# Gate and up projections of two feed-forwards as seven block products, with gate and down in two phases

## The chip, the cores and the metric

One core of a Trainium2 chip. The metric is device time in microseconds (us) from one launch; lower is better.

## The reference

One step of a small backbone of two layers over 1024 latent tokens and 128 context tokens, width 1024. Layer 0 mixes tokens by differential attention, layer 1 by a long convolution (Hyena). Behind each mixer's output projection stands a feed-forward:

```
h = rmsnorm(x) * g * (1 + scale) + shift
x = x + gate * ((silu(h @ w_g) * (h @ w_u)) @ w_down)
```

with w_g and w_u of 1024 x 2816 and w_down of 2816 x 1024. Everything is float32. scale, shift and gate come from a second set of products ("ada") with the condition vectors, one set for latents, one for context. At the end stands one more rmsnorm.

## The kernel before, in words

Activations lie transposed: 128 partitions hold 128 of the 1024 features, so a tensor is 8 blocks (k) of 1152 tokens. The tokens are worked in NCH = 3 chunks of CH = 384 columns, mostly in the order 2, 0, 1 (`ORDER`); the context is the last 128 columns of chunk 2.

Each float32 operand is split into a high and a low part of the fp32r type, and a product is three matmuls: high x high, high x low, low x high (`three`, L289). `lin` (L294) runs these over the 8 blocks of features: 24 matmuls for one output block of 128 x 384. A weight unit of 512 KB is loaded by `fetch` (L271) into one of two `raw` buffers through SP's queue; ScalarE copies it to the high part (L279) and VectorE subtracts for the low part (L280), three buffers each. `part` (L1311) does the same for other operands, `split` (L462) with GpSimd for the high part.

`project` (L835) is the mixer's output projection: eight output blocks d, for each of the three chunks one `lin` and a `residual` (L824: x += gate * PSUM, on VectorE), followed by the square of x on ScalarE (L398) and its sum over the blocks on GpSimd (L402). The last three units are worked chunk by chunk, and `step` normalises a chunk while the next one is multiplied: `rstd` (L407) sums over partitions on TensorE, takes the square root on ScalarE, refines it in five small VectorE operations, spreads it by three products with a diagonal (L430, L431); `modulate` (L434) multiplies each block with it (L444), scales it on ScalarE (L446) and splits it (L447, L448). The last chunk's step stands inside `ffn`, behind the first products of chunk 2.

`ffn` (L866) runs over the HT = 22 tiles of hidden features. For each tile and chunk `gated` (L1116) makes the gate block and the up block (one `lin` each), silu on ScalarE (L1124), the product on VectorE (L1125) and the split on GpSimd and VectorE (L463, L464). After each second tile the two are multiplied with w_down and the 8 output blocks of each chunk are added to x; the last four tiles are summed in PSUM first. So gate, up and down are interleaved, and activations of the hidden layer never leave SBUF. In layer 0 the ada products of layer 1 (`ada_step`, L344, four loads of 512 KB in two buffers, 32 small matmuls) stand one behind each of the tiles 2 to 13.

The order of instructions on an engine is chosen by a planner of the framework from the program's order and its own estimate of times, SP's queue of DMAs included; `pin` (L632) fixes the program's order on the engines that it names for a stretch. It is used in the attention and in the convolution, not in the feed-forwards.

## Time and profile before

| | us |
|---|---|
| median of three runs | 3223.13 |
| lowest, highest run | 3221.38, 3225.62 |
| span of the profiled execution | 3218.2 |
| TensorE busy in it | 3140.6 |
| VectorE busy | 1702.0 |
| ScalarE busy | 1006.4 |
| GpSimd busy | 672.8 |

The page lists no own time for the profiled execution, so its span stands beside the median of the runs, which is 4.9 us longer. The feed-forward of layer 0 lies at about 985 to 1815 us of the span, that of layer 1 at 2387 to 3200. A matmul's record overlaps the next one's, so its cost is read from the distance of two starts. GpSimd stands as POOL, VectorE as DVE, ScalarE as ACT, TensorE as PE and its weight loads as PEld.

### The profile page before, as it was taken

Reading aid. Unit: us, or ns where it says so; the run is one execution under the profiler, and the core shown is the slowest. Engines: PE = TensorE matmul, PEld = TensorE weight load, DVE = VectorE, ACT = ScalarE, POOL = GpSimd, SP = SyncE. Lnnn points to the kernel's source line nnn. Section 1 sums busy time; section 2 is a strip of 40 time slices with the busy share of each in tenths; the row PEclk is TensorE's granted clock in tenths of the full one; section 3 lists DMA queues with packets and bytes.
Section 4 is the critical chain, followed back from the end, with each engine's and each line's share of the span. In section 5 each row is a group of like instructions: output and inputs, shape, how many; then the busy total and the mean of one; then the engine's idle time right before and its main releaser. Section 6 shows DMA issues by size and latency. Waiting matters only on the chain.

```text
span 3218.2 us, 49673 instructions
## 1 busy us (share of the span) xinstructions
PE 3140.6 (98%) x20266; PEld 3069.1 (95%) x20266; DVE 1702.0 (53%) x2902; ACT 1006.4 (31%) x1892; POOL 672.8 (21%) x739
## 2 busy tenths in 40 slices
PE   6899999999999999999999999999999999999998
PEld 5779989999999999999999999999999999999998
DVE  7866524989736333333432578875453344444324
ACT  3541124888624111111111442335451111111114
POOL 5844401444332000000000413132230000000003
PEclk9899999999999999999999999999999999999999
DMA  6565452444211222222111233345401111111111
GB/s 251 203 217 178 139 161 63 101 97 101 92 40 60 92 92 92 92 92 79 40 53 40 101 118 114 124 169 196 141 34 46 40 47 46 40 40 40 51 42 66
DMA packets 123084, 308.13 MB, mean 96 GB/s; under 512 B 12991, under 2 KB 65607, under 8 KB 118760
## 3 DMA queue, kind: packets, MB, share of 16 engines
q1 hardware_dynamic: 107480, 282.58, 26.7%
q10 hardware_dynamic: 13968, 17.65, 1.6%
q0 software_dynamic: 1408, 4.72, 0.4%
q8 instruction: 160, 2.62, 0.3%
q14 instruction: 68, 0.56, 0.1%
HBM read 243.56 MB, written 61.34 MB: 95 GB/s over the span
## 4 chain that ended last, share of the span: by engine, by line
PE 88%; DMA 4%; DVE 3%; POOL 1%; issue 1%; ACT 1%; SPq 0%; ACTq 0%; POOLq 0%; DVEq 0%
PE mm L290 25%; PE mm L291 25%; PE mm L292 25%; PE tr L770 4%; PE sc L744 2%; PE sc L745 2%; PE tr L761 2%; PE tr L353 1%; DMA zt<-d_z 1%; DVE wl L915 1%; PE tr L292 1%; PE tr L290 1%; PE tr L291 1%; DMA pr<-d_p 0%; DMA kk<-d_k 0%
## 5 line engine op out<-in xcount | busy, mean ns | idle before, releaser
L291 PE MATMUL mm<-hl,wh 128*128 128x384 f32 x3408 | 1140.2, 335 | 0.9 <-DVE hl L507 0.8
L290 PE MATMUL mm<-hh,wh 128*128 128x384 f32 x3408 | 1137.8, 336 | 2.4 <-ACT hh L506 1.8
L292 PE MATMUL mm<-hh,wl 128*128 128x384 f32 x3408 | 1137.3, 335 | 0.0
L290 PEld LDWEIGHTS mm<-hh,wh 128*128 128x128 f32 x3408 | 639.7, 188 | 8.1 <-ACT hh L506 2.7
L291 PEld LDWEIGHTS mm<-hl,wh 128*128 128x128 f32 x3408 | 640.3, 188 | 4.6 <-issue 1.8
L292 PEld LDWEIGHTS mm<-hh,wl 128*128 128x128 f32 x3408 | 640.2, 188 | 1.9 <-issue 0.4
L279 ACT ACTIVATE wh<-raw 128x1024 fp32r<-128x1024 f32 x194 | 203.5, 1058 | 950.3 <-PE mm L291 827.0
L827 DVE SCALAR_TENSOR_TENSOR x<-mm,ada,x 128x256 f32<-128x256 f32 (+1 forms) x704 | 343.2, 513 | 278.0 <-PE mm L292 276.8
L1125 DVE TENSOR_TENSOR silu<-mm,silu 128x384 f32<-128x384 f32 x132 | 73.5, 557 | 593.9 <-PE mm L292 589.4
L463 POOL TENSOR_SCALAR ah<-silu 128x384 fp32r<-128x384 f32 x132 | 70.3, 533 | 1462.3 <-DVE silu L1125 1449.8
L280 DVE TENSOR_TENSOR wl<-raw,wh 128x1024 fp32r<-128x1024 f32 x194 | 243.9, 1265 | 214.5 <-ACT wh L279 214.3
L291 PE MATMUL mm<-al,wh 128*128 128x384 f32 x1056 | 354.1, 335 | 0.0
L290 PE MATMUL mm<-ah,wh 128*128 128x384 f32 x1056 | 353.8, 335 | 0.0
L292 PE MATMUL mm<-ah,wl 128*128 128x384 f32 x1056 | 353.3, 335 | 0.0
L1124 ACT ACTIVATE silu<-mm 128x384 f32<-128x384 f32 x132 | 64.0, 485 | 440.6 <-PE mm L292 440.6
L291 PEld LDWEIGHTS mm<-al,wh 128*128 128x128 f32 x1056 | 198.3, 188 | 1.4 <-issue 1.2
L290 PEld LDWEIGHTS mm<-ah,wh 128*128 128x128 f32 x1056 | 198.3, 188 | 1.2 <-issue 1.2
L292 PEld LDWEIGHTS mm<-ah,wl 128*128 128x128 f32 x1056 | 198.3, 188 | 0.0
L751 DVE TENSOR_REDUCE nm<-sc 128x1 f32<-128x1152 f32 x128 | 173.5, 1356 | 33.4 <-PE sc L745 33.3
L753 ACT ACTIVATE pr<-sc,nm 128x1152 f32<-128x1152 f32 x128 | 156.7, 1224 | 14.0 <-DVE nm L751 7.7
L402 POOL TENSOR_TENSOR nacc<-nacc,nsq 128x384 f32<-128x384 f32 x104 | 117.0, 1129 | 182.8 <-ACT nsq L398 182.1
L744 PE MATMUL sc<-kk,qs 128*128 128x384 f32 x384 | 140.0, 364 | 3.3 <-ACT pr L753 3.3
(300 smaller groups left out, 4228.0 us busy)
## 6 DMA issues: line engine op xcount, KB each, us to landing
raw<-w_gu SPq DMA_DIRECT2D x88, 512.0 KB, 3.3
araw<-ada_w SPq DMA_DIRECT2D x64, 512.0 KB, 4.1
kk<-d_k SPq DMA_DIRECT2D x16, 1152.0 KB, 8.4
raw<-w_down SPq DMA_DIRECT2D x36, 512.0 KB, 3.7
raw<-w_in SPq DMA_DIRECT2D x24, 512.0 KB, 3.2
hl<-ada_w SPq DMA_DIRECT2D x23, 512.0 KB, 7.4
d_f<-bf ACTq DMA_DIRECT2D x16, 512.0 KB, 2.6
raw<-w_qk SPq DMA_DIRECT2D x16, 512.0 KB, 5.8
```

The lines of the kernel that those rows point to most:

```text
L279: nc.scalar.activation(hi, raw, AF.Copy)
L280: nc.vector.tensor_tensor(out=lo, in0=raw, in1=hi.bitcast(F32), op=ALU.subtract)
L290: self.nc.tensor.matmul(out, ah, bh, start=first, stop=False)
L291: self.nc.tensor.matmul(out, ah, bl, start=False, stop=False)
L292: self.nc.tensor.matmul(out, al, bh, start=False, stop=last)
L402: nc.gpsimd.tensor_tensor(out=self.acc[c], in0=self.acc[c], in1=sq, op=ALU.add)
L744: nc.tensor.matmul(sc[:, c, :CH], lhs, kk[:, 0, p, ks], start=True, stop=False)
L751: nc.vector.tensor_reduce(out=nm, in_=sv, axis=AX.XY, op=ALU.max, negate=True)
L753: nc.scalar.activation(e.rearrange("p (a b) -> p a b", a=3), sv, AF.Exp, bias=nm, accum_out=st[hd][3][:, p, qt : qt + 1])
L770: self.nc.tensor.matmul(po[:, :P], at[:, b], v[:, b], start=b == 0, stop=b == 8)
L827: self.nc.vector.scalar_tensor_tensor(out=x[:, d, s:e], in0=ps[:, s:e], scalar=gate[:, d, g : g + 1], in1=x[:, d, s:e], op0=ALU.mult, op1= ...
L1125: nc.vector.tensor_tensor(out=s, in0=pu[:, :CH], in1=s, op=ALU.mult)
```

## The change

The gate tile and the up tile of one t are taken as the two block rows of a 2 x 2 block matrix (features k 0 to 3 and 4 to 7 are its block columns), and the tokens in two halves of HALF = 576 columns as the block columns of the other factor, k 0 to 3 and 4 to 7 as its block rows. Their product is made by Winograd's form of Strassen's scheme: seven block products instead of eight, each over 4 blocks k and in two parts of SUB = 288 columns, with sums of the weights (on GpSimd, `side_sums`), sums of the tokens (`combos`, once for a feed-forward) and sums of the products (on VectorE, out of PSUM). P1 is the product of the gate's first half with the tokens' first half, and so on, by the numbers in `mul`. The order of TensorE, VectorE, ScalarE and GpSimd is pinned for the whole phase.

x is written to DRAM (`d_r`) by the projection and normalised in place; each hidden tile is written to DRAM (`d_a`). Then a second phase, `down`, loads x and, in groups of 2, 4, 4, 4, 4, 4 tiles, the hidden tiles, splits them and multiplies with w_down. The 12 ada steps go to that phase, one behind each weight unit from the second group on. x is now held in half rows of 576 tokens (16 tiles `xk`), so chunk 1 lies in two of them and its operations are done in two pieces; the output projection takes the chunks in the order 0, 1, 2. The 16 `xk` buffers also serve for the weight sums and the products' sums while gate and up are made, and the space of h serves for the tokens' combinations.

```
+HALF = NT // 2
+SUB = HALF // 2
+GROUPS = [2, 4, 4, 4, 4, 4]
...
+    def open_h(self, tags=("hs", "hs")):
+        self.hstack = ExitStack()
+        self.hp = self.hstack.enter_context(self.pool("h"))
+        self.htags = tags
+
+    def htile(self, shape, dt=F32, which=0):
+        return self.tl(self.hp, shape, dt, tag=self.htags[which], bufs=6 if self.htags[0] == self.htags[1] else 3)
...
     def load_x(self, src):
-        self.x = []
-        for c in range(NCH):
-            t = self.tl(self.xp, [P, KT, CH], tag=f"x{c}")
-            self.nc.sync.dma_start(t, src[c])
-            self.x.append(t)
+        self.xk = []
+        for k in range(KT):
+            self.xk.append([])
+            for h in range(2):
+                t = self.tl(self.xp, [P, HALF], tag="xk", bufs=16)
+                self.nc.sync.dma_start(t, src[k][:, HALF * h : HALF * h + HALF])
...
+        a, sh = self.scales(l, 1)
+        low = [self.operand(bx, f"b{j}") for j in range(2)]
+
+        def step(c):
+            rs = self.rstd(c)
+            for k in range(KT):
+                for x, s, e, _ in self.whole(c, k):
+                    nc.vector.tensor_tensor(out=x, in0=rs[:, s:e], in1=x, op=ALU.mult)
+                for x, s, e, g in self.x(c, k):
+                    nc.scalar.activation(x, x, AF.Identity, scale=a[:, k, g : g + 1], bias=sh[:, k, g : g + 1])
+                if c < 2:
+                    o = slice(0, CH) if c == 0 else slice(CH, HALF)
+                    self.part(*(t[:, k % 4, o] for t in low[k // 4]), self.xk[k][0][:, o])
+
...
+                    for x, s, e, _ in self.whole(c, d):
+                        nc.sync.dma_start(self.d_r[l][d][:, CH * c + s : CH * c + e], x)
+                    if d == 5 and c:
+                        step(c - 1)
...
+    def operand(self, pool, tag):
+        return tuple(self.tl(pool, [P, 4, HALF], F32R, tag=tag + n) for n in "hl")
+
+    def combos(self, low, bx, tp):
+        nc, tt = self.nc, self.tt
+        ADD, SUB = ALU.add, ALU.subtract
+        t1, t2, t3 = (self.operand(tp, f"t{j}") for j in range(1, 4))
+        top = self.operand(bx, "b2")
+        u, v = (self.tl(tp, [P, 4, HALF], tag="t4" + n) for n in "hl")
+        f = lambda t, k: t[:, k].bitcast(F32)
+        b = [self.xk[k][1] for k in range(KT)]
+        self.ops = ops = {1: low[0], 2: low[1], 3: top, 5: t1, 6: t2, 7: t3}
+
+        def second():
+            for k in range(4):
+                tt(u[:, k], b[k], f(low[0][0], k), SUB)
+                tt(u[:, k], u[:, k], f(low[0][1], k), SUB)
+                tt(v[:, k], b[k + 4], u[:, k], SUB)
+                self.part(t2[0][:, k], t2[1][:, k], v[:, k])
+
+        def third():
+            for k in range(4):
+                tt(b[k], b[k + 4], b[k], SUB)
+                self.part(t3[0][:, k], t3[1][:, k], b[k])
+
+        def first():
+            for k in range(4):
+                self.part(t1[0][:, k], t1[1][:, k], u[:, k])
+
+        def fourth():
+            for k in range(4):
+                tt(b[k], f(low[1][0], k), v[:, k], SUB, nc.gpsimd)
+                tt(b[k], b[k], f(low[1][1], k), ADD, nc.gpsimd)
+            t4 = ops[4] = self.operand(tp, "t4")
+            for k in range(4):
+                self.part(t4[0][:, k], t4[1][:, k], b[k])
+
+        def last():
+            for k in range(4):
+                self.part(top[0][:, k], top[1][:, k], b[k + 4])
+
+        return second, third, first, fourth, last
+
+    def side_load(self, l, t):
+        raws = [self.tl(self.wp, [P, 1024], tag="raw", bufs=2) for _ in range(2)]
+        for raw, at in zip(raws, (t, HT + t)):
+            self.nc.sync.dma_start(raw, self.i["w_gu"][l, at])
+        return raws
+
+    def side_sums(self, g, u):
+        nc, tt = self.nc, self.tt
+        ADD, SUB = ALU.add, ALU.subtract
+        s1, s2, s3, s4 = (self.tl(self.xp, [P, 512], tag="xk", bufs=16) for _ in range(4))
+        a11, a12, a21, a22 = g[:, 0:512], g[:, 512:1024], u[:, 0:512], u[:, 512:1024]
+        tt(s1, a21, a22, ADD, nc.gpsimd)
+        tt(s2, s1, a11, SUB, nc.gpsimd)
+        tt(s3, a11, a21, SUB, nc.gpsimd)
+        tt(s4, a12, s2, SUB, nc.gpsimd)
+        return s1, s2, s3, s4
+
+    def side_one(self, x):
+        w = tuple(self.tl(self.xp, [P, 512], F32R, tag="xk", bufs=16) for _ in range(2))
+        self.part(*w, x)
+        return w
+
+    def side_two(self, *src):
+        hi, lo = (self.tl(self.wp, [P, 1024], F32R, tag=n, bufs=3) for n in ("wh", "wl"))
+        for j, y in enumerate(src):
+            c = slice(0, 1024) if len(src) == 1 else slice(512 * j, 512 * j + 512)
+            self.part(hi[:, c], lo[:, c], y)
+        return (hi[:, 0:512], lo[:, 0:512]), (hi[:, 512:], lo[:, 512:])
+
+    def times(self, out, w, b, first):
+        wh, wl = (y.rearrange("p (k c) -> p k c", c=P) for y in w)
+        for k in range(4):
+            for h in range(2):
+                c = slice(SUB * h, SUB * h + SUB)
+                self.three(out[:, h, 0:SUB], wh[:, k], wl[:, k], b[0][:, k, c], b[1][:, k, c], first and k == 0, k == 3, skip_group_check=True)
+
+    def gate_up(self, l, combos):
+        nc, tt, ops = self.nc, self.tt, self.ops
+        st = {t: {"w": {}} for t in range(HT + 1)}
+
+        def raws(t):
+            if t < HT:
+                st[t]["raw"] = self.side_load(l, t)
+
+        def sums(t):
+            if t < HT:
+                st[t]["s"] = self.side_sums(*st[t]["raw"])
+
+        def pair(t, n):
+            if t < HT:
+                w = st[t]["w"]
+                if n == 1:
+                    w[1], w[2] = self.side_two(st[t]["raw"][0])
+                elif n == 2:
+                    w[6], w[7] = self.side_two(*st[t]["s"][1:3])
+                elif n == 3:
+                    w[5], w[3] = self.side_two(*st[t]["s"][0::3])
+                else:
+                    w[4] = self.side_one(st[t]["raw"][1][:, 512:1024])
+
+        def bank():
+            return self.tl(self.pp, [P, 2, 512], tag="pr", bufs=3)[:, :, 0:SUB]
+
+        def work():
+            return self.tl(self.xp, [P, 2, SUB], tag="xk", bufs=16)
+
+        def mul(t, n):
+            q, name, first = st[t], {1: "a", 2: "a", 6: "b", 5: "b", 3: "b", 7: "c", 4: "c"}[n], n in (1, 6, 7)
+            if first:
+                q[name] = bank()
+            self.times(q[name], q["w"][n], ops[n], first)
+
+        def p1(t):
+            mul(t, 1)
+            st[t]["s1"] = work()
+            nc.scalar.activation(st[t]["s1"], st[t]["a"], AF.Copy)
+
+        def p2(t):
+            mul(t, 2)
+            st[t]["g"] = work()
+            nc.scalar.activation(st[t]["g"], st[t]["a"], AF.Silu)
+
+        def p6(t):
+            q = st[t]
+            mul(t, 6)
+            q["v"] = work()
+            tt(q["v"], q["b"], q["s1"], ALU.add)
+
+        def p7(t):
+            q = st[t]
+            mul(t, 7)
+            q["r"] = work()
+            tt(q["r"], q["c"], q["s1"], ALU.add)
+
+        def p5(t):
+            q = st[t]
+            mul(t, 5)
+            tt(q["r"], q["b"], q["r"], ALU.add)
+
+        def p4(t):
+            q = st[t]
+            mul(t, 4)
+            tt(q["v"], q["c"], q["v"], ALU.add)
+            tt(q["v"], q["g"], q["v"], ALU.mult, nc.gpsimd)
+            nc.sync.dma_start(self.d_a[l][t][:, 0:HALF], q["v"].rearrange("p a b -> p (a b)"))
+
+        def p3(t):
+            q = st[t]
+            mul(t, 3)
+            tt(q["s1"], q["b"], q["s1"], ALU.add)
+            nc.scalar.activation(q["s1"], q["s1"], AF.Silu)
+            tt(q["r"], q["s1"], q["r"], ALU.mult, nc.gpsimd)
+            nc.sync.dma_start(self.d_a[l][t][:, HALF:NT], q["r"].rearrange("p a b -> p (a b)"))
+            del st[t]
+
+        second, third, first, fourth, last = combos
+        raws(0), sums(0), pair(0, 1), pair(0, 4), raws(1), pair(1, 1)
+        p1(0), p1(1)
+        pair(0, 2), second()
+        p2(0), p2(1)
+        pair(0, 3)
+        p6(0), third()
+        p7(0), first()
+        p5(0), fourth(), sums(1), pair(1, 2), pair(1, 4), raws(2)
+        p4(0), last()
+        p3(0), pair(1, 3)
+        for t in range(1, HT):
+            if t > 1:
+                pair(t, 3)
+                p1(t)
+            sums(t + 1), pair(t + 1, 4)
+            p6(t)
+            if t > 1:
+                p2(t)
+            p7(t), pair(t + 1, 1)
+            p5(t), pair(t + 1, 2), raws(t + 2) if t + 2 < HT else None
+            p4(t)
+            p3(t)
+
+    def ffn(self, l, after):
+        bx, tp, ps = ExitStack(), ExitStack(), ExitStack()
+        bp = bx.enter_context(self.pool("bx", side="right"))
+        low, step = self.project(l, bp)
+        self.hstack.close()
+        tpool = tp.enter_context(self.pool("tp"))
+        step(NCH - 1)
+        self.mstack.close()
+        self.pp = ps.enter_context(self.pool("psa", space=bass.MemoryType.PSUM))
+        start = len(self.nc.cur_bb.bb.instructions)
+        self.at += 1
+        self.gate_up(l, self.combos(low, bp, tpool))
+        self.pin(start, (ENG.PE, ENG.DVE, ENG.Activation, ENG.Pool))
+        ps.close()
+        self.open_mm()
+        tp.close()
+        bx.close()
+        self.open_h()
+        self.load_x(self.d_r[l])
+        self.bstack = ExitStack()
+        self.ntp = self.sp = self.bstack.enter_context(self.pool(f"ffn{l}", side="right"))
+        return self.down(l, after)
+
+    def down(self, l, after):
         nc = self.nc
         gate = self.gate(l, 1)
...
+        at, ada, step = 0, 0, None
+
+        def load(at, m):
+            act = [self.htile([P, 2, 4, CH], F32R) for c in range(NCH)]
+            for k in range(m):
+                raw = self.tl(self.sp, [P, NT], tag="araw2", bufs=3)
+                nc.sync.dma_start(raw, self.d_a[l][at + k])
+                for c in range(NCH):
+                    self.part(act[c][:, 0, k], act[c][:, 1, k], raw[:, CH * c : CH * c + CH])
+            return act
+
+        acts = [load(0, GROUPS[0])]
+        for n, m in enumerate(GROUPS):
+            last = n == len(GROUPS) - 1
+            act = acts.pop(0)
+            at += m
+            if not last:
+                acts.append(load(at, GROUPS[n + 1]))
+            if last:
+                step = after()
+            per = D * m // 1024
+            for us in ([0], [1, 2, 3]) if last else [[u] for u in range(per)]:
+                ws = self.weights(3) if len(us) == 3 else [self.weights()]
                 for c in ORDER:
...
+                    for u, w in zip(us, ws):
+                        w = [y.rearrange("p (k d) c -> p k d c", k=m) for y in w]
+                        for e in range(8 // per):
+                            d = 8 // per * u + e
+                            ps = self.mm()
+                            for k in range(m):
+                                self.three(ps[:, :CH], w[0][:, k, e], w[1][:, k, e], act[c][:, 0, k], act[c][:, 1, k], k == 0, k == m - 1)
+                            self.residual(ps, d, c, gate, last)
+                            if last and d == 2 and c != ORDER[0]:
+                                step()
+                if l == 0 and n and ada < 12:
+                    self.ada_step(1, ada)
+                    ada += 1
         return step
```

## Rows read from the trace of the kernel before

**Rows 1.** The page: span, then busy time (share) and instructions of each engine.

```profile
span 3218.2 us, 49673 instructions
...
PE 3140.6 (98%) x20266; PEld 3069.1 (95%) x20266; DVE 1702.0 (53%) x2902; ACT 1006.4 (31%) x1892; POOL 672.8 (21%) x739
```

**Rows 2.** Stretches: us, busy (count) by engine, clock, DMA share, GB/s.

```profile
core 0: us, PE busy (x) PEld busy (x) DVE busy (x) ACT busy (x) POOL busy (x), PEclk, DMA share, GB/s
985.00:1790.00 805.00, 804.35 (x5246) 792.80 (x5245) 305.37 (x528) 116.01 (x173) 44.50 (x75) 1.00 0.21 72
2387.00:3155.00 768.00, 768.00 (x4437) 768.00 (x4436) 299.48 (x510) 111.52 (x159) 43.53 (x74) 1.00 0.12 42
...
0.00:200.00 200.00, 161.78 (x1293) 138.15 (x1294) 161.96 (x266) 94.09 (x171) 125.05 (x144) 0.95 0.62 222
```

**Rows 3.** TensorE's waits in 985 to 1815: us, times, longest.

```profile
PE tr L353 <- DMA araw<-ada_w: 0.6, 1, 0.6
```

**Rows 4.** Timeline of TensorE, first down product: start us, us, instruction.

```profile
2599.85 0.33 PE L290 MATMUL mm<-ah,wh 128*128 128x384 f32 x1
...
2601.41 0.33 PE L290 MATMUL mm<-ah,wh 128*128 128x384 f32 x1
```

**Rows 5.** Timeline of TensorE, values projection.

```profile
449.89 0.28 PE L290 MATMUL mm<-wh,hh 128*128 128x256 f32 x1
...
450.97 0.28 PE L290 MATMUL mm<-wh,hh 128*128 128x256 f32 x1
```

**Rows 6.** Groups by line and form, weight loads: busy us, mean ns.

```profile
L290 PEld LDWEIGHTS mm<-hh,wh 128*128 128x128 f32 x3408 | 639.7, 188 | 8.1 <-ACT hh L506 2.7 <-issue 2.2 <-POOL hh L810 1.0
...
L290 PEld LDWEIGHTS mm<-wh,hh 128*128 128x128 f32 x288 | 55.8, 195 | 0.8 <-issue 0.2
```

**Rows 7.** Groups by line and form, VectorE; then its timeline.

```profile
L280 DVE TENSOR_TENSOR wl<-raw,wh 128x1024 fp32r<-128x1024 f32 x194 | 243.9, 1265 | 214.5 <-ACT wh L279 214.3
...
L444 DVE TENSOR_TENSOR nt<-tr,x 128x384 f32<-128x384 f32 x72 | 37.1, 548 | 6.2 <-PE tr L431 3.9 <-POOL hl L448 1.7
...
974.02 1.22 DVE L280 TENSOR_TENSOR wl<-raw,wh 128x1024 fp32r<-128x1024 f32 x1
...
981.50 1.94 DVE L444 TENSOR_TENSOR nt<-tr,x 128x384 f32<-128x384 f32 x4
```

**Rows 8.** Groups by line and form, ScalarE; then its timeline.

```profile
L279 ACT ACTIVATE wh<-raw 128x1024 fp32r<-128x1024 f32 x194 | 203.5, 1058 | 950.3 <-PE mm L291 827.0 <-issue 108.9 <-DMA raw<-w_gu 6.5
...
L447 ACT ACTIVATE hh<-nt 128x384 fp32r<-128x384 f32 x72 | 35.9, 513 | 0.2
...
974.97 0.97 ACT L446 ACTIVATE nt<-nt,ada,A 128x256 f32<-128x256 f32 x2
```

**Rows 9.** Groups by line and form, GpSimd operations with two operands.

```profile
L627 POOL TENSOR_TENSOR pr<-pr,pr 128x384 f32<-128x384 f32 x64 | 63.9, 999 | 5.0
...
L915 POOL TENSOR_TENSOR gt<-zt,gt 128x1024 f32<-128x1024 f32 x7 | 16.8, 2399 | 35.7 <-DVE zt L1360 35.7
```

**Rows 10.** Timeline of VectorE, start of the second feed-forward.

```profile
2396.29 0.16 DVE L420 TENSOR_SCALAR nv<-tr 128x3 f32<-128x3 f32 x1 [1.21 <-ACT nr L419]
...
2397.50 0.48 DVE L430 TENSOR_SCALAR ndg<-ident,nr 128x128 f32<-128x128 f32 x2
...
2403.14 0.56 DVE L444 TENSOR_TENSOR nt<-tr,x 128x384 f32<-128x384 f32 x1 [0.29 <-PE tr L431]
```

**Rows 11.** Timelines of VectorE and GpSimd, start of the first feed-forward.

```profile
975.15 0.55 DVE L448 TENSOR_TENSOR hl<-nt,hh 128x384 fp32r<-128x384 f32 x1
...
978.24 1.38 DVE L448 TENSOR_TENSOR hl<-nt,hh 128x384 fp32r<-128x384 f32 x1
...
978.20 1.01 POOL L402 TENSOR_TENSOR nacc<-nacc,nsq 128x384 f32<-128x384 f32 x1
979.17 1.33 POOL L448 TENSOR_TENSOR hl<-nt,hh 128x384 fp32r<-128x384 f32 x1
```

**Rows 12.** TensorE's longest wait on a load in v(); stretches around it.

```profile
PE aux L600 <- DMA pr<-d_p: 6.7, 1, 6.7
...
438.90:449.20 10.30, 5.82 (x28) 5.59 (x29) 1.41 (x7) 2.34 (x8) 0.00 (x0) 0.50 0.71 210
449.20:460.00 10.80, 10.80 (x91) 10.55 (x91) 1.71 (x8) 2.88 (x11) 0.00 (x0) 1.00 0.20 66
```

**Rows 13.** DMA issues: kernel tile, source, queue, count, KB each, us to landing.

```profile
raw<-w_gu SPq DMA_DIRECT2D x88, 512.0 KB, 3.3
araw<-ada_w SPq DMA_DIRECT2D x64, 512.0 KB, 4.1
...
raw<-w_down SPq DMA_DIRECT2D x36, 512.0 KB, 3.7
```

229 lines of the change are left out of this document (95 added, 134 removed).

## The prediction

> **What bounds the kernel now.** I read the engines' totals first: TensorE is busy for 3140.6 of 3218.2 us, VectorE for 1702 [rows 1]. Then the two feed-forwards by stretch: in 805 us and in 768 us TensorE has practically no gap, while VectorE is busy for under 40%, ScalarE under 15% and GpSimd under 6% [rows 2], and the waits of TensorE in the first of them come to 0.6 us, once [rows 3]. So nothing but matmul time is worth anything there, and any wait that the change puts in front of TensorE is paid in full. What one matmul costs is read from starts, since their durations overlap: nine matmuls of 384 columns lie between 2599.85 and 2601.41 us, 173.3 ns each [rows 4]; nine of 256 columns between 449.89 and 450.97, 120.0 ns each [rows 5]. The difference is 53.3 ns for 128 columns, so a matmul costs 0.4167 ns a column and 13.3 ns besides; 288 columns cost 133.3 ns. A weight load's record is 188 ns at 384 columns and 195 ns at 256 [rows 6], and yet the matmuls of 256 follow each other every 120 ns: loads are no limit there, nor between the two.
>
> **Part 1, seven products for eight.** Before, gate and up are 22 tiles x 2 x 3 chunks x 8 k x 3 = 3168 matmuls of 384 columns for each feed-forward: 549.0 us. After, 22 x 7 products x 4 k x 2 halves x 3 = 3696 matmuls of 288: 492.8 us. The columns fall by an eighth, but 528 matmuls more each bring their 13.3 ns. Saved: 56.2 us, twice, **112.4 us**. The down product keeps its 1584 matmuls of 384 columns: 0.
>
> **Part 2, a tile in the steady state.** One product is 24 x 133.3 ns = 3.2 us, a tile 22.4 us. Prices: VectorE takes 0.55 us for 384 elements and 1.22 to 1.27 for 1024, and 1.94 for four of 384 in a row [rows 7], so about 0.6 for 512 and 0.67 for 576 in a row; ScalarE 0.51 for 384 and 1.06 for 1024 [rows 8], 0.53 and 0.58; GpSimd's two-operand operations 1.00 for 384 and 2.40 for 1024 [rows 9], 1.28 and 1.42. Per tile VectorE has weight splits of 1.2 + 5 x 0.6 and five sums out of PSUM at 0.7: 7.7 us; ScalarE about 6; GpSimd the four weight sums and two gate products, 4 x 1.28 + 2 x 1.42 = 8.0, which it now does in a written order. Each result is needed a product or more (3.2 us) after it can be made. DMA moves 1.6 MB a tile, 73 GB/s; the first 200 us moved 222 GB/s at a share of 0.62 [rows 2]. The removed gate steps (silu, product, split of three chunks) and 96 residual adds were hidden too. Cost 0; if that cover went, each microsecond a tile would be 44 us.
>
> **Part 3, the start of each feed-forward.** Before, the last chunk's normalisation is covered by matmuls of another chunk. Now the right half of the tokens enters five of the seven products, and TensorE's order is fixed, so it has only P1 and P2 of two tiles, 4 x 3.2 = 12.8 us, as cover. I count from the projection's last matmul. What comes first is the norm: square, sum on GpSimd, square root, five small VectorE steps, the diagonal products; from 2396.29 to the first normalised block at 2403.14 is 6.9 us [rows 10], and residual, square and sum before it are about 2. Then ScalarE scales eight blocks in two pieces, 0.97 us a pair [rows 8]; the first combination wants five of them: 13 us at the earliest. On ScalarE that combination also stands behind the copy of P1 of tile 1, whose weights wait for a raw buffer that GpSimd's four sums hold: up to 24. I take 18. From there VectorE makes 36 operations of 576 (24.1 us); in eight of the blocks it waits for ScalarE's half of the split (8 x 0.78 = 6.2); five weight halves (3.0) and four sums out of PSUM (2.8) stand between them in the fixed order, and the sums wait for the ends of four products (about 6): 42 us. GpSimd meanwhile has the eight operations of the fourth combination and four weight sums, 16.5 us. The two slow each other: a split of 384 took 0.55 us alone and 1.38 with GpSimd at a tensor operation beside it, and GpSimd's next one 1.33 instead of 1.00 [rows 11]. I put half of the 16.5 on the path, 8. The Trainium skill (SBUF — State Buffer, SBUF: two separate sides) goes further: a VectorE operation with two SBUF inputs and a GpSimd operation lock each other out entirely; the trace agrees in kind, and by that rule all 16.5 us would count, 8.5 more each time, 3226 us in all. The last product of tile 0 then ends at 18 + 42 + 8 + 1 = 69 us, and nine products fill 28.8 of them: **40 us** idle, with ends at 13 + 42 + 1 - 28.8 = 27 and 24 + 42 + 16.5 + 1 - 28.8 = 55. To it comes the clock: in the 10.3 us from 438.9 the granted clock was 0.50 (1.2 GHz), around a wait of 6.7 us for a load; TensorE was busy for 5.8 of them, and the clock was full again once it had worked on [rows 12]. In the new start TensorE works in bursts of 0.8 us. At half clock a product takes 24 x (240 + 13) ns = 6.1 us by the slope above (an estimate); three whole ones and two tails late would be 10 us. I take 3, ends 0 and 10. Twice 43 is **86 us**.
>
> **Part 4, from gate and up to down.** The first down matmuls need two tiles back from DRAM, split, and a weight split. Buffers for all of them come free 3 to 19 us before the last product ends (P1, P2, P5 are done by then), a load lands in 3.3 to 3.7 us [rows 13], four splits of 384 need 2: if SP issues these loads early, TensorE loses nothing. The 16 loads of x are wanted 1 us later at the first residual, the others over 25 us. But SP's queue also has the last tile's two stores, and what stands behind them waits for the last product, a VectorE sum, silu and GpSimd's product, about 3 us, then load and split, 5. Ends 0 and 8 us if that is all; I take 4, twice **8 us**.
>
> **Part 5, the rest.** The 12 steps of the second layer's modulation move to the down phase, one for each 12.5 us (72 matmuls of 173.3 ns) instead of one a tile. Each brings four loads of 512 KB on SP into two buffers, 4.1 us each [rows 13]: 8 to 9 us, hidden if the planner spaces the matmuls that wait for them; with acts and weights 3.1 MB in 12.5 us, 250 GB/s, near what the first 200 us show [rows 2]. 0 to 12 us, I take 3. The 32 stores of x from each projection and the order of chunks 0, 1, 2 are behind matmuls: 0. Chunk 1 now is two pieces everywhere, and it is the last of the final step: 1 us. The first x loads in rows of 1.5 KB: 0, the path there is elsewhere.
>
> **Sum.** 3218.2 - 112.4 + 86 + 8 + 3 + 1 = 3203.8 us of span. The median of the runs, 3223.1, is 4.9 above that execution's span; added again: **3209 us**, 0.4% less than before. Its ends: with 27, 0, 0, 0 it is 3165; with 55 and 10 for a start, 8 and 12 it is 3270.
>
> **Rivals.** *(a) The start is shorter:* VectorE hardly meets GpSimd and the first combination starts at 13 us: 27 us each and nothing for the clock. Then 3223.1 - 112.4 + 54 + 8 + 3 + 1 = 3177. For it: most VectorE operations of 384 to 1024 in these rows run at their undisturbed time [rows 7]; against it: GpSimd's sums fall exactly into this stretch. *(b) The start is dearer:* the meeting with GpSimd takes all 16.5 us [rows 11] and the clock stays low: 8.5 + 7 more each, 3209 + 31 = 3240. For it speak the rows [rows 11, 12], and the rule of that page speaks for the first half of it; against it, that half of GpSimd's work falls into VectorE's own waits. *(c) Slower by SP's queue:* if the 16 loads of x (4.7 MB, 21 us at the 222 GB/s of the first 200 us [rows 2]) are issued ahead of the loads of tiles and stand behind the last stores, the down phase starts 3 + 21 + 5 = 29 us after the last product, 25 more than I count, twice: 3259. It decides from about 11 us each on, where the forecast's gain is gone. For it: SP serves in order and the x loads come first in the program; against it: the loads of weights before show them running ahead, with 0.6 us of wait in 805. *(d) The change doesn't do what it says:* a product costs more than its matmuls, say 0.3 us at each change of bank, 308 times, 92 us: 3301. Against it: waits of that kind are not seen where the kernel now changes bank every 24 matmuls [rows 3].
>
> **Chances.** Forecast 0.42, (a) 0.28, (b) 0.13, (c) 0.12, (d) 0.05. About 0.2%, 6.4 us, can be told from no change here: 3216.7 to 3229.5 is the same. The forecast's own range is 3190 to 3230: of its 0.42 some 0.27 are faster, 0.13 the same, 0.02 slower. With (a) faster is 0.55; the same is 0.15 with 0.02 of (b); slower 0.30 with the rest. Range for 8 in 10: 3165 (the end of (a)) to 3250, which leaves out (d) and most of (c).
>
> **What would show it.** Gate and up matmuls every 133 ns, a steady tile of 22.4 us without a wait; TensorE's waits in the first tile of each feed-forward on VectorE's low parts of t2, t3, t1 and t4, together near 40 us; VectorE's splits there over 0.7 us while GpSimd works; a gap under 8 us before the first down matmul. Wrong would be a pitch above 140 ns, a wait in every tile, or a start or handover outside the ends above.

## The result and the profile after

| | before | after |
|---|---|---|
| median, us | 3224.4 (4 runs, 3221.4 to 3226.7) | 3246.6 (4 runs, 3244.5 to 3253.2) |
| ratio after : before, 95% interval | | 1.0074 [1.0059, 1.0088] |
| span of the profiled execution | 3218.2 | 3251.4 |
| TensorE busy in it | 3140.6 | 3081.2 |

The kernel became 0.7% slower; 0.4% faster was forecast. The time is inside the range, near its upper end, on the other side of the kernel before. The page of the kernel after, where [rows 1] stood before:

```profile
span 3251.4 us, 53225 instructions
...
PE 3081.2 (95%) x21322; PEld 2988.6 (92%) x21322; DVE 1946.7 (60%) x3139; ACT 1183.5 (36%) x2284; POOL 1012.0 (31%) x866
```

TensorE has 59 us less to do and the span is 33 us longer (the profiled execution is the slowest of the four; the medians differ by 22): the work went, and waits came. Where they are is seen in the stretches of the first feed-forward, against [rows 2] (columns: us, busy time and count of each engine, granted clock, DMA share, GB/s):

```profile
core 0: us, PE busy (x) PEld busy (x) DVE busy (x) ACT busy (x) POOL busy (x), PEclk, DMA share, GB/s
...
1000.00:1060.00 60.00, 39.46 (x169) 32.71 (x169) 39.05 (x43) 21.81 (x37) 21.04 (x12) 0.66 0.03 9
1085.00:1531.00 446.00, 446.00 (x3363) 446.00 (x3362) 216.45 (x218) 112.47 (x178) 176.65 (x117) 1.00 0.23 79
1532.00:1541.00 9.00, 0.28 (x1) 0.28 (x2) 3.10 (x9) 3.06 (x6) 1.86 (x1) 0.72 1.04 410
```

In the steady part TensorE is busy all the time at the full clock of 2.4 GHz, 3363 matmuls in 446 us, 132.6 ns each. In 60 us of the start it gets through 169 matmuls instead of some 450, at a mean granted clock of 0.66. In 9 us between gate/up and down it does one.

By stage, from the two traces: the first feed-forward, from the last values product of the attention to the first product behind it, takes 973.7 us instead of 960.1 (13.6 more), the second 959.8 instead of 949.2 (10.6 more), the stages between them 1.9 more. Another 7.0 us lie before 547 us, where the change does little: in the thirteen traces of this study that keep the change's first stages the first product of the values starts anywhere between 538.9 and 549.8 us, so a single execution can differ by as much from that alone. The experiments are therefore read by stage, from the start of the projection's last matmul (T): to the first combination, to the start of the last matmul of tile 0's last product, to that of the last product of gate and up, and from there the gap to the first down matmul. Kernels with the same start agree in these within 2 us, so a difference below that is not told apart from none.

| kernel | first combination starts, after T | tile 0's last product | gate and up in all | gap to down |
|---|---|---|---|---|
| after, layer 0 / layer 1 | 29.7 / 29.5 | 87.8 / 87.3 | 551.6 / 550.5 | 9.1 / 9.0 |
| forecast | 18 | 69 (72 with the clock) | 535.8 | 4 |

TensorE's waits in the start (us, times, longest):

```profile
PE pr L305 <- ACT wh L1550: 6.5, 1, 6.5
PE pr L305 <- ACT t3h L1550: 6.1, 3, 4.0
PE pr L305 <- ACT t2h L1550: 4.8, 3, 2.0
PE pr L306 <- DVE t4l L1551: 2.5, 3, 1.3
```

The longest is for weights (P1 of tile 1), the others for parts of the combinations and of the other token operands. What these in turn wait for is in the timelines of ScalarE, VectorE and GpSimd (start us, us, instruction, in brackets the idle time before it and what ended it):

```profile
999.45 1.04 ACT L1550 ACTIVATE wh<-raw 128x1024 fp32r<-128x1024 f32 x1
...
1007.35 0.65 ACT L1035 ACTIVATE xk<-pr 128x576 f32<-128x576 f32 x1 [3.69 <-PE pr L307]
1007.89 1.14 ACT L1550 ACTIVATE wh<-xk 128x512 fp32r<-128x512 f32 x2
...
1009.76 0.75 DVE L1165 TENSOR_TENSOR t4h<-xk,b0h 128x576 f32<-128x576 f32 x1
...
1012.85 0.76 DVE L1551 TENSOR_TENSOR t2l<-t4l,t2h 128x576 fp32r<-128x576 f32 x1 [0.75 <-ACT t2h L1550]
...
1033.77 1.95 DVE L1165 TENSOR_TENSOR xk<-xk,xk 128x576 f32<-128x576 f32 x1
...
1043.70 4.14 DVE L1551 TENSOR_TENSOR t1l<-t4h,t1h 128x576 fp32r<-128x576 f32 x4
1051.05 0.76 DVE L1165 TENSOR_TENSOR xk<-pr,xk 128x576 f32<-128x576 f32 x1 [3.21 <-PE pr L307]
1051.72 4.94 DVE L1551 TENSOR_TENSOR t4l<-xk,t4h 128x576 fp32r<-128x576 f32 x4
...
1061.21 3.96 DVE L1551 TENSOR_TENSOR b2l<-xk,b2h 128x576 fp32r<-128x576 f32 x4
...
1031.37 1.86 POOL L1165 TENSOR_TENSOR xk<-b1h,t4l 128x576 f32<-128x576 f32 x1 [37.03 <-DVE t3l L1551]
```

Four causes offer themselves. The first combination (t4h, 1009.76) stands in the pinned order behind the split of tile 1's gate weights, P1 of tile 1, its copy and the split of P6's weights. In each block VectorE stands 0.75 us for ScalarE's half. With GpSimd at work, VectorE's operations take 1.95 instead of 0.75, and four splits 4.0 to 4.9 instead of 2.7. And sums of products stand ahead of splits in VectorE's order and wait for TensorE, which waits for splits.

### The profile page after: what moved, and what is told of

It is laid out like the page before. It is cut to its first block, busy times and chain, and to the rows that moved or that the text cites. A ratio compares the mean times of both kernels' runs of the same rounds, so it can differ in the third digit from the quotient of the medians.

```text
span 3251.4 us, 53225 instructions
## 1 busy us (share of the span) xinstructions
PE 3081.2 (95%) x21322; PEld 2988.6 (92%) x21322; DVE 1946.7 (60%) x3139; ACT 1183.5 (36%) x2284; POOL 1012.0 (31%) x866
## 4 chain that ended last, share of the span: by engine, by line
PE 80%; DVE 6%; DMA 4%; ACT 2%; issue 2%; POOL 1%; SPq 0%; POOLq 0%; ACTq 0%; DVEq 0%
PE mm L305 13%; PE mm L306 13%; PE mm L307 12%; PE pr L306 10%; PE pr L307 10%; PE pr L305 10%; PE tr L785 4%; PE sc L759 2%; PE tr L776 2%; PE sc L760 2%; PE tr L368 1%; PE tr L307 1%; PE tr L305 1%; PE tr L306 1%; ACT xk L891 1%
## 5 line engine op out<-in xcount | busy, mean ns | idle before, releaser
L305 PE MATMUL mm<-hs,wh 128*128 128x384 f32 x1824 | 611.3, 338 | 17.5 <-ACT hs L1550 17.5
L306 PE MATMUL mm<-hs,wh 128*128 128x384 f32 x1824 | 614.2, 337 | 0.4 <-POOL hs L463 0.3
L307 PE MATMUL mm<-hs,wl 128*128 128x384 f32 x1824 | 612.5, 336 | 0.0
L857 DVE SCALAR_TENSOR_TENSOR xk<-mm,ada,xk 128x192 f32<-128x192 f32 (+3 forms) x560 | 233.3, 453 | 335.5 <-PE mm L307 329.8
L1165 DVE TENSOR_TENSOR xk<-pr,xk 128x576 f32<-128x576 f32 x220 | 166.0, 755 | 424.8 <-PE pr L307 228.2
L305 PEld LDWEIGHTS mm<-hs,wh 128*128 128x128 f32 x1824 | 343.5, 189 | 23.1 <-ACT hs L1550 18.0
L306 PEld LDWEIGHTS mm<-hs,wh 128*128 128x128 f32 x1824 | 344.2, 189 | 4.2 <-issue 1.8
L307 PEld LDWEIGHTS mm<-hs,wl 128*128 128x128 f32 x1824 | 344.0, 189 | 2.2 <-issue 0.8
L1551 DVE TENSOR_TENSOR wl<-xk,wh 128x512 fp32r<-128x512 f32 x176 | 196.1, 1153 | 71.3 <-ACT wh L1550 70.8
L305 PE MATMUL mm<-hh,wh 128*128 128x384 f32 x576 | 193.5, 339 | 3.3 <-ACT hh L521 2.8
L306 PE MATMUL mm<-hl,wh 128*128 128x384 f32 x576 | 194.9, 338 | 0.7 <-DVE hl L522 0.7
L307 PE MATMUL mm<-hh,wl 128*128 128x384 f32 x576 | 194.7, 338 | 0.0
```

Source lines behind the costliest of these rows:

```text
L305: self.nc.tensor.matmul(out, ah, bh, start=first, stop=False, **kw)
L306: self.nc.tensor.matmul(out, ah, bl, start=False, stop=False, **kw)
L307: self.nc.tensor.matmul(out, al, bh, start=False, stop=last, **kw)
L857: self.nc.vector.scalar_tensor_tensor(out=x, in0=ps[:, s:e], scalar=gate[:, d, g : g + 1], in1=x, op0=ALU.mult, op1=ALU.add)
L1165: (eng or self.nc.vector).tensor_tensor(out=o, in0=a, in1=b, op=op)
L1551: self.nc.vector.tensor_tensor(out=lo, in0=x, in1=hi.bitcast(F32), op=ALU.subtract)
```

## The experiments

**The gap to the down phase.** At the end of gate and up, in the kernel after:

```profile
1531.63 0.29 PE L307 MATMUL pr<-b2h,wl 128*128 128x288 f32 x1
...
1521.85 6.24 SPq L838 DMA_DIRECT2D xk<-d_r  x10
...
1529.28 1.06 SPq L838 DMA_DIRECT2D xk<-d_r  x2
...
1531.52 0.42 SPq L838 DMA_DIRECT2D xk<-d_r  x1
1532.24 1.81 SPq L1131 DMA_DIRECT2D araw<-d_a  x3
...
1539.32 2.78 ACT L1550 ACTIVATE hs<-araw 128x384 fp32r<-128x384 f32 x6 [5.86 <-DMA araw<-d_a]
```

SP issues the loads of the first hidden tiles (araw) 0.6 us after the last product starts its last matmul, behind 13 loads of x. Is it the order in the queue, or the space? The addresses that the program gives its buffers speak for the space: the second tile's buffer (bytes 164,544 to 169,152 of each partition) overlaps b2h (165,056 to 174,272), the operand of P3, which is the last product (the next expectation calls it the third combination, after P3). In the second feed-forward the buffers of both first tiles overlap b2h. First run, other buffers:

```
+            got.append(self.tl(self.xp, [P, HALF], tag="xk", bufs=16))
+            self.nc.sync.dma_start(got[-1], self.d_a[l][t][:, HALF * h : HALF * h + HALF])
...
+        self.early = [self.side_back(l, t) for t in range(GROUPS[0])]
         self.load_x(self.d_r[l])
```

> Theory, the buffers: the 9.1 and 9.0 us between the last product and the first down matmul arise because the loads of the first two hidden tiles go into buffers that lie in the space of the tokens' third combination, which the last product still reads; SP can issue them only after it. Here those two tiles come into four of the half-row buffers, which are free 10 us earlier, so both gaps should fall to 1 to 3 us and the time by 12 to 16 us, to about 3232. Rival, the queue: SP serves the loads of x and the last stores first in any case, or the split waits for space too; then the gaps stay at 7 to 9 us and the time at 3246 (within 4).

Measured: 3234.0 us (the kernel before beside it 3222.7), gaps of 0.13 and 0.14 us. Its timeline:

```profile
1533.26 0.29 PE L307 MATMUL pr<-b2h,wl 128*128 128x288 f32 x1
1533.39 0.34 PE L305 MATMUL mm<-hs,wh 128*128 128x384 f32 x1
...
1523.48 1.85 SPq L1127 DMA_DIRECT2D xk<-d_a  x4
...
1530.38 0.53 ACT L1569 ACTIVATE hs<-xk 128x384 fp32r<-128x384 f32 x1 [5.37 <-DMA xk<-d_a]
```

The loads go out 10 us before the end, the split begins 3 us before it, and the whole 9 us are gone, twice. Second run, the same buffers as after, with the call that loads the hidden tiles ahead of the one that loads x:

```
-        self.load_x(self.d_r[l])
...
         acts = [load(0, GROUPS[0])]
+        self.load_x(self.d_r[l])
```

> The same buffers as after the change, but the program asks for the first two hidden tiles ahead of the 16 loads of x. Theory, the buffers: SP can't issue those loads before the last product has read the space that they go to, so the two gaps stay at 8 to 10 us and the time within 5 us of 3246. Rival, the queue (the loads of x ahead of them, as the third rival of the prediction has it): the gaps fall to under 5 us and the time to about 3236.

Measured: 3244.8 us (before 3222.3), gaps of 9.2 and 9.4 us. The planner, which orders SP's queue, put the loads where they had been, 0.7 us behind the last product's last matmul. So the order of the calls changes nothing, and another space for the data changes everything. What another order in SP's queue would do with the same space was not run.

**When the first combination starts.** First the raw buffer: the up weights of tile 0 go into t4l's space, which is still free, and tile 1's gate weights are loaded early.

```
-                st[t]["raw"] = self.side_load(l, t)
+                up = self.free if t == 0 else None
+                st[t]["raw"] = self.side_load(l, t, up)
```

> Theory, the raw buffer: the first combination starts 29.5 us after the projection's last matmul because the load of tile 1's gate weights waits for the raw buffer that GpSimd's four sums of tile 0 hold. Here the up weights of tile 0 lie elsewhere and tile 1's gate weights are loaded early, so P1 of tile 1 should follow P1 of tile 0 without the 6.8 us gap, and the first combination should start at 20 to 23 us; each start 7 to 9 us shorter, the time about 3231. Rival, ScalarE: its scaling of the last chunk (it ends at 1003.7) and the splits behind it bound the first combination; then it moves by under 4 us and the time by under 8.

Measured: 3245.3 us (before 3222.7). The load came early, but the first combination starts at 28.7 and 28.4, tile 0's last product ends at 85.0 and 86.6: the rival's size, 3 and 1 us, little more than two equal starts differ by. A wait of TensorE and VectorE's timeline show what stands in the place of the load:

```profile
PE pr L307 <- DVE wl L1555: 5.2, 1, 5.2
```

```profile
995.06 1.21 DVE L1555 TENSOR_TENSOR wl<-raw,wh 128x1024 fp32r<-128x1024 f32 x1
```

P1 of tile 1 waits in its middle for the low half of its weights, which the pinned order puts behind another split, that of P4's weights; by then VectorE is busy with the last chunk's normalisation, until 994.5. So a further run keeps the early load and puts that split second:

```
-        raws(0), sums(0), pair(0, 1), pair(0, 4), raws(1), pair(1, 1)
+        raws(0)
+        st[1]["raw"] = [self.side_half(l, 1)]
+        pair(0, 1), pair(1, 1), sums(0), pair(0, 4)
+        st[1]["raw"].append(self.side_half(l, HT + 1))
```

> As the run with the up weights of tile 0 elsewhere, and the split of tile 1's gate weights now stands second in the pinned order, ahead of GpSimd's sums and of the split of P4's weights. Theory, the order: in that earlier run P1 of tile 1 still waited 5.2 us for the low half of its weights, which VectorE made behind the last chunk's normalisation; split early, P1 of tile 1 runs at 13.4 us, its copy no longer holds ScalarE, and the first combination starts at 20 to 21.5 us instead of 29.5; each start is 7 to 9 us shorter than after the change. Rival: ScalarE's scaling and the split of P6's weights hold the first combination beyond 25 us, and the start gains under 4 us each.

Measured: 3239.0 us (before 3228.0). P1 of tile 1 runs from 13.4, the first combination starts at 21.4 and 22.8, tile 0's last product ends at 80.7 and 80.1: 7 us shorter each. This chain, and not the load alone, held VectorE. ScalarE's and VectorE's timelines there:

```profile
998.80 0.63 ACT L1044 ACTIVATE xk<-pr 128x576 f32<-128x576 f32 x1
999.33 1.14 ACT L1562 ACTIVATE wh<-xk 128x512 fp32r<-128x512 f32 x2
...
1001.19 0.75 DVE L1177 TENSOR_TENSOR t4h<-xk,b0h 128x576 f32<-128x576 f32 x1
```

The copy of P1 and the split of P6's weights are the same two as at 1007.35 and 1007.89 after the change, some 8 us earlier.

**GpSimd beside VectorE.** Its eight operations of the fourth combination are left out.

```
-            for k in range(4):
-                tt(b[k], f(low[1][0], k), v[:, k], SUB, nc.gpsimd)
-                tt(b[k], b[k], f(low[1][1], k), ADD, nc.gpsimd)
```

> Left out: GpSimd's eight operations that make the fourth combination of the tokens in each feed-forward (P4 then multiplies with the third combination's values), so its output is another. Theory, the shared port: beside them the block of the third combination takes 3.75 us instead of 2.15 and the splits behind it 1.0 to 1.2 us instead of 0.7, all on the path of the start; without them each start is 7 to 9 us shorter, the time about 3231. Rival: VectorE waits for ScalarE and for the products anyway; then the third combination's block is shorter but the last product of tile 0 ends within 3 us of where it did, and the time is within 6 us of 3246.

Measured: 3236.7 us (before 3222.7); tile 0's last product ends at 82.1 and 83.5, 5.7 and 3.8 earlier: between the two expectations. VectorE's operations are at once as short as alone:

```profile
1028.79 0.75 DVE L1162 TENSOR_TENSOR xk<-xk,xk 128x576 f32<-128x576 f32 x1
...
1033.38 2.76 DVE L1548 TENSOR_TENSOR t1l<-t4h,t1h 128x576 fp32r<-128x576 f32 x4
```

With nothing left out, but the eight made by VectorE:

```
-                tt(b[k], f(low[1][0], k), v[:, k], SUB, nc.gpsimd)
-                tt(b[k], b[k], f(low[1][1], k), ADD, nc.gpsimd)
+                tt(b[k], f(low[1][0], k), v[:, k], SUB)
+                tt(b[k], b[k], f(low[1][1], k), ADD)
```

> The change with one edit: the eight operations of the fourth combination are made by VectorE instead of GpSimd, nothing left out. Theory: left out altogether they were worth 5.9 and 3.7 us; on VectorE they cost 8 times 0.67 to 0.76, that is 5.4 to 6.1, of which its waits for products hide up to 3: each start ends within 3 us of 87.5. Rival, the lock costs more than the work: each start is 4 us shorter or more.

Measured: 3256.8 us (before 3228.0), tile 0's last product at 88.4 and 89.3: 0.6 and 2.0 later, no more than equal starts differ by. In this order of work the two prices cancel.

**The clock.** Matmuls with unused results in TensorE's waits.

```
+            for _ in range(warm[k]):
+                self.nc.tensor.matmul(self.spare, self.ops[1][0][:, 0, 0:P], self.ops[1][0][:, 0, 0:CH], start=True, stop=True)
```

> Added: matmuls of 384 columns with unused results, 179 for each feed-forward, put in the waits of TensorE in the first tile (24 ahead of P1 of tile 1, 44 in P6, 58 in P7, the others in P5, P4 and P3). Theory, the clock: the granted clock stays at 2.4 GHz there, P5, P4 and P3 of tile 0, now 6.5 to 8.3 us each, take 3.5 to 5, and each start is 6 to 9 us shorter: about 3232. Rival, VectorE's chain: the clock is full but these products then wait for the splits of t1, t4 and b2; the last product of tile 0 ends within 3 us of where it did, the time is within 6 us of 3246, or some us longer where the added matmuls are in the way.

Measured: 3241.2 us (before 3222.7), tile 0's last product at 86.4 and 87.8: 1.5 earlier and 0.5 later. A stretch of the start in the kernel after, from P6 to P5 of tile 0, at a granted clock of 0.50 (1.2 GHz):

```profile
1017.00:1051.00 34.00, 20.96 (x67) 16.31 (x66) 22.28 (x25) 12.30 (x19) 14.20 (x8) 0.50 0.00 0
```

and, with the added matmuls, from the end of P6 through P7 into P5, at 1.00 (2.4 GHz):

```profile
1018.00:1037.00 19.00, 14.89 (x87) 13.53 (x86) 14.48 (x14) 6.02 (x10) 13.98 (x8) 1.00 0.00 1
```

P7 takes 11.6 us there and 12.0 in the kernel after: at either clock it waits for t3. Three other products differ. P1 of tile 1 in layer 0 takes 4.1 us at 1.00 with the added matmuls ahead of it, instead of 6.4 at 0.51, and the first combination starts at 27.4 instead of 29.7. P5 and P3 the run can't price: the added matmuls take TensorE's time themselves (8 in P5, 19 in P3), and the mean clock in the two was still 0.80 and 0.81. The kernel after shows it; the first two rows are the second and the last matmul of P5, the others the fourth block's first low product and the last matmul of P4:

```profile
1044.67 0.61 PE L306 MATMUL pr<-t1l,wh 128*128 128x288 f32 x1 [1.45 <-DVE t1l L1551]
...
1050.57 0.44 PE L307 MATMUL pr<-t1h,wl 128*128 128x288 f32 x1
...
1056.71 0.40 PE L306 MATMUL pr<-t4l,xk 128*128 128x288 f32 x1 [0.70 <-DVE t4l L1551]
...
1057.35 0.29 PE L307 MATMUL pr<-t4h,xk 128*128 128x288 f32 x1
```

At 0.50 the matmuls of P5 follow each other every 0.24 us, slower than the splits of t1 come, and the last starts 2.7 us behind the last of these splits (43.70 + 4.14); in P4, at 0.97, it starts 0.7 us behind that of t4. P3, at 0.61, ends 2.7 us behind the last split of b2. So the low clock costs, by an estimate from these rows, 2 us in P5, on whose end VectorE waits, and 2 in P3.

**VectorE's own chain.** The low halves of t2 and t3 one step later, and the third combination ahead of the sum of P6.

```
         def second():
             for k in range(4):
                 tt(u[:, k], b[k], f(low[0][0], k), SUB)
+                if k:
+                    lower(t2, k - 1, v[:, k - 1])
...
-        p6(0), third()
+        third(), pair(0, 3)
+        p6(0)
```

> The VectorE half of each split of the second and third combination is put one step later, so that VectorE doesn't stand 0.75 us for ScalarE's half in each block, and the third combination goes ahead of the sum of P6. Theory, VectorE's chain sets the start: a block of the second combination takes 3.0 us instead of 3.76, of the third 1.5 to 3 instead of 2.15 to 3.75, the last product of tile 0 ends 5 to 8 us earlier in each feed-forward, the time about 3233. Rival: what follows (the splits of t1, t4 and b2 behind sums of products, at half clock) waits for something else, and the gain is under 2 us each.

Measured: 3234.7 us (before 3222.3); tile 0's last product at 81.9 and 79.4, 5.9 and 7.9 earlier. Both edits of this run are in these gains. A block of the second combination takes 2.98 us (from 1009.94 to 1012.92) instead of 3.76, and the low half of t2, now inside the next block, stands for nothing:

```profile
1009.94 0.75 DVE L1178 TENSOR_TENSOR t4h<-xk,b0h 128x576 f32<-128x576 f32 x1
1010.78 0.76 DVE L1178 TENSOR_TENSOR t2l<-t4l,t2h 128x576 fp32r<-128x576 f32 x1
...
1012.92 0.75 DVE L1178 TENSOR_TENSOR t4h<-xk,b0h 128x576 f32<-128x576 f32 x1
```

**Seven products against eight in the same frame.**

```
+        def gate(t, h):
+            st[t]["g", h] = self.tl(self.xp, [P, 2, SUB], tag="xk", bufs=16)
+            nc.scalar.activation(st[t]["g", h], prod(t, 0, h), AF.Silu)
+
+        def up(t, h):
+            y = st[t]["g", h]
+            tt(y, prod(t, 1, h), y, ALU.mult)
...
+            gate(t, 0), prep(t + 1, 0), gate(t, 1)
+            up(t, 0), prep(t + 1, 1), raws(t + 2), up(t, 1)
```

> The change without its seven products: the same two phases, halves of 576 columns, matmuls of 288 columns and handover, but eight block products for each tile and no sums of weights or tokens; the right half of the tokens is only split. Theory: a product costs its 24 matmuls of 132.7 ns, so 22 more of them cost 70 us in each feed-forward; the start needs no combinations and leaves TensorE idle for about 12 us instead of 59. Gate and up together then take about 572 us from the projection's last matmul instead of 551, the time is about 3289. Rival: the sums of the seven products cost TensorE more than this (or the start's wait is not theirs), and the eight come to 551 or less, the time to 3246 or below.

Measured: 3279.0 us (before 3222.3); gate and up together 573.2 and 573.0 us, and behind them gaps of 2.6 and 5.9. The first feed-forward's stretches, start, steady part and gap:

```profile
973.70:1016.20 42.50, 34.63 (x236) 33.64 (x236) 25.07 (x59) 26.82 (x57) 2.83 (x2) 0.88 0.18 56
1016.20:1546.80 530.60, 530.60 (x4009) 530.60 (x4008) 80.71 (x83) 67.28 (x84) 0.00 (x0) 1.00 0.23 74
1546.90:1549.40 2.50, 0.28 (x3) 0.04 (x1) 2.02 (x7) 2.30 (x4) 0.00 (x0) 1.00 0.45 109
```

The eight come to 4224 matmuls of 132.6 ns, 560 us, and 13 us of waits. The seven cost 551 instead of 573: of the 70 us that an eighth of the matmuls is worth (528 x 132.6 ns), 48 go into the wait for their combinations. Against the kernel before, even the frame without the seven products costs 27 to 30 us in each feed-forward: 11 for matmuls of 288 columns instead of 384 (560 against 549), 13 of start, 3 to 6 of gap.

**All of it together:** the half-row buffers, the early load and split, the halves one step later, and, new, the combinations ahead of the products' sums in VectorE's order:

```
         p1(0), p1(1)
-        pair(0, 2), second()
-        p2(0), p2(1)
-        pair(0, 3)
-        p6(0), third()
-        p7(0), first()
-        p5(0), fourth(), sums(1), pair(1, 2), pair(1, 4), raws(2)
-        p4(0), last()
+        second(), third(), pair(0, 2)
+        p2(0), p2(1)
+        first(), pair(0, 3), p6(0)
+        fourth(), p7(0)
+        sums(1), last(), p5(0)
+        p4(0)
+        pair(1, 2), pair(1, 4), raws(2)
```

> The change with the two hidden tiles in half-row buffers (gap 0.1 us), the up weights of tile 0 elsewhere, the splits one step later, the combinations ahead of the sums of products in VectorE's order, and the weights of tile 1 behind them. Theory, the start is a chain of VectorE and its waits: the first combination starts at 20 to 23 us, the last product of tile 0 ends at 64 to 72 us instead of 87.5, and the time is 3246 - 18 - 2 x 16 to 23 = 3182 to 3196. Rival, contention and the clock: VectorE's work next to GpSimd and TensorE at 1.2 GHz eat most of it, the last product ends at 78 to 84 us and the time is 3210 to 3220.

Measured: 3199.2 us (before 3222.3), faster than either kernel, but not as far as the theory said. The first combination starts at 19.5 and 19.9 and tile 0's last product ends at 70.7 and 70.4, as expected; TensorE now waits 18.1 and 16.5 us for P6's weights, whose split this order put behind the third combination. VectorE's and GpSimd's timelines where they meet:

```profile
1016.56 1.95 DVE L1209 TENSOR_TENSOR t3l<-xk,t3h 128x576 fp32r<-128x576 f32 x1
...
1018.44 1.95 DVE L1209 TENSOR_TENSOR xk<-xk,xk 128x576 f32<-128x576 f32 x1
1020.31 3.82 DVE L1209 TENSOR_TENSOR t3l<-xk,t3h 128x576 fp32r<-128x576 f32 x2
...
1038.29 6.44 DVE L1595 TENSOR_TENSOR b2l<-xk,b2h 128x576 fp32r<-128x576 f32 x4
...
1017.98 1.79 POOL L1209 TENSOR_TENSOR xk<-xk,b1l 128x576 f32<-128x576 f32 x1
1019.73 1.91 POOL L1209 TENSOR_TENSOR xk<-b1h,t4l 128x576 f32<-128x576 f32 x1
1021.72 1.79 POOL L1209 TENSOR_TENSOR xk<-xk,b1l 128x576 f32<-128x576 f32 x1
```

In these rows to 1024 VectorE is never idle, and it gets through exactly one operation for each of GpSimd's, one pair each 1.9 us, close to the 2.1 that 0.67 and 1.4 make one after the other; the split of b2 stands beside GpSimd's weight sums. So the next two runs take GpSimd away from there. The first moves P6's weights into the second combination and the fourth combination to VectorE:

```
-        second(), third(), pair(0, 2)
+        second(lambda: pair(0, 2)), third()
```

> The kernel with all mends, and besides: the weights of P6 are split inside the second combination (P6 waited 18 us for them), and the fourth combination is made by VectorE instead of GpSimd. Theory, contention: VectorE's ten operations beside GpSimd's fourth combination took 15.4 us there and would take 6.7 alone; eight operations of 0.67 to 0.76 more on VectorE cost 5.4 to 6.1, so VectorE gains about 3 us, and TensorE 3 to 10 by the earlier P6: last product of tile 0 at 58 to 67 us, time 3178 to 3192. Rival: VectorE has no free time there, its chain grows by the 6 us, and the time is 3199 to 3210.

Measured: median 3186.8 us of four runs, against 3225.4 of seven of the kernel before: ratio 0.9880 [0.9864, 0.9897]. Tile 0's last product ends at 67.2 and 66.9. The second makes the weight sums of tile 1 on VectorE too:

```
-        last(), sums(1), p5(0)
-        p4(0)
+        last(), p5(0)
+        sums(1, nc.vector), p4(0)
```

> As the run before, and the four weight sums of tile 1 are made by VectorE too, so that GpSimd does nothing beside the splits. Theory, contention: the split of b2 beside these sums took 6.44 us instead of 2.75 and the next three operations 3.9 instead of 2.8, for four sums that cost VectorE 2.4 to 2.8 us; the last product of tile 0 ends 2 to 4 us earlier than in the run before, the time is 4 to 8 us shorter. Rival: the sums now stand in VectorE's order ahead of the products' sums; no gain or up to 6 us longer.

Measured: median 3180.1 us, ratio 0.9864 [0.9849, 0.9878]; tile 0's last product at 65.6 and 64.1, 1.6 and 2.8 earlier. VectorE's split of b2, and the stretches of start and steady part:

```profile
1029.43 2.76 DVE L1597 TENSOR_TENSOR b2l<-xk,b2h 128x576 fp32r<-128x576 f32 x4
```

```profile
972.60:1038.40 65.80, 44.56 (x238) 40.43 (x237) 60.02 (x107) 38.58 (x78) 9.90 (x7) 0.74 0.06 21
1038.40:1501.20 462.80, 461.88 (x3480) 461.68 (x3479) 229.74 (x233) 119.76 (x193) 186.24 (x122) 1.00 0.24 81
```

VectorE is busy for 60 of the 66 us: the start is now its work, no longer its waits. This version takes 2.0% less time than the change as it was and 1.4% less than the kernel before.

## Why the prediction was wrong, step by step

*Part 1 held.* 132.6 ns a matmul against the 133.3 forecast from [rows 4, 5]: 3696 of them take 490 us instead of 492.8. *Part 2 held:* no wait in the steady tiles. With that rival (d) is out.

*Part 3 failed, at two terms.* Forecast were 40 us idle and 3 for the clock in each start; it was 59 (87.8 - 28.8, and 58.5). The first term is the sentence "I take 18" for the first combination: it started at 29.7 and 29.5, and this is most of the miss. The mechanism was named there, the copy of P1 of tile 1 behind weights that wait for a raw buffer, and priced at "up to 24"; what the price left out is that P1 of tile 1 then takes 6.4 us at the half clock, that its copy and one more weight split stand in between, and that the early load alone would not have helped (28.7 with it, 21.4 with the split in another place too).

The second is the chain of 42 us. From the first combination to the last product lie 58 us, against 51 forecast with port and end. VectorE's timeline divides them, in the first feed-forward: 42.3 us of operations, 6.0 of waits for ScalarE's halves, 4.9 for the ends of P7 and P5 (1.7 and 3.2), 2.3 for ScalarE ahead of the split of P5's weights, and 2.7 from the last split of b2 to the last matmul. The halves were forecast at 6.2, the other waits at 6, the end at 1; the operations at 29.9, and 8 for GpSimd. In the run without the fourth combination's eight operations on GpSimd VectorE's take 37.4, so these cost 5.0. The rows beside GpSimd's weight sums and first gate product (t4l, the weights' wl and b2l: 4.94, 3.28 and 3.96 us, undisturbed 2.76, 1.29 and 2.76) hold another 5. GpSimd's share is then some 10 and not 8, and VectorE's own work some 32 and not 29.9. The 3 for the clock was too little as well: 2.3 us ahead of the first combination by the run with added matmuls (1.0 in the second feed-forward), and by the estimate above 4 more, which lie inside the wait for P5 and the end.

The Trainium skill (SBUF — State Buffer, SBUF: two separate sides) says that a VectorE operation with two SBUF inputs and a GpSimd operation hold the shared port for a whole instruction, one excluding the other. The one-for-one rows of the run with all mends nearly agree with that: a pair each 1.9 us, 0.2 less than the two in sequence. The prediction's reading of it, that all 16.5 us of GpSimd's work would then count, doesn't follow: where VectorE waits for something else anyway, GpSimd's turn costs nothing, and the run without the fourth combination's operations, some 11 us of GpSimd, gained 4 to 6.

*Part 4 failed.* Forecast 4 with an upper end of 8, measured 9.1 and 9.0. The step is the sentence that buffers for all the loads come free 3 to 19 us before the last product, "P1, P2, P5 are done by then": the second tile's buffer lies in the space of P3's operand, and P3 is the last product. It was a statement about addresses that I had not looked up. What then follows, load and split, was sized at 5 and took 8.5: 7.1 from the issue to the first split, with all DMA engines busy (a share of 1.04 in those 9 us), and 1.4 for the split.

*Part 5* can't be told from the spread of single traces.

Sum of the misses: 2 x 16 for the starts, 2 x 5 for the gaps, less 2 x 2.7 for the matmuls, some 37 us; the medians differ from the forecast by 3246.6 - 3209 = 37.6.

*The rivals.* (b) gave 3240, the nearest number, and its start, 18 + 42 + 16.5 + 1 + 10 - 28.8 = 58.7 us idle, is nearly the measured 59, but by luck: GpSimd comes to some 10 us instead of 16.5 and the clock to some 6 by estimate instead of 10, and the late first combination, which (b) doesn't have, makes up for both. (c), the queue, is out in the form given: the gap is 9 us, not 29, the order of the calls doesn't matter, the space does. (a) would have needed what the last runs made by hand, and even they reach only 64 to 67 us, not 56.

## What to carry to other kernels

A scheme that saves matmuls pays at its seams: count what must be ready before the first new product, follow the pinned order of each engine back from it, and put work that waits for TensorE behind work that TensorE waits for. When a pool is closed and another opened in its space, look up which old tile each new buffer overlaps and who reads that tile last; here 18 us hung on where small buffers lay. And where two engines share a port, the price of moving work between them depends on whether either has idle time there: the same edit was worth nothing in one order of work, and in another it was one of two edits that together took over 3 us off each start.

## What had not been expected of the hardware

VectorE and GpSimd, both without a break on tensor operations with SBUF operands, alternate one instruction for one instruction, though alone they take 0.67 to 0.76 and 1.40 to 1.45 us: from 1016 to 1026 us of the run with all mends a pair takes 1.9 us, so that VectorE runs at under half its pace. An operation of VectorE that needs the result of the one before it starts 0.79 us behind it (1009.76 and 1010.55 after the change), while the four splits of b2 in the last run start 0.67 apart; why is not shown. And what the half clock costs depends on the wait beside it: nothing much where a product waits for operands to its end (P7 took 12.0 us at a granted clock of 0.50 and 11.6 at 1.00), and some 2 us, by the estimate above, where operands come faster than its matmuls run, as in P5.
